# The down product of a feed-forward block as seven block products instead of eight

## The chip, the core and the metric

The kernel runs on one core of a Trainium2 chip. A core has a matrix engine (TensorE, PE in the profile), a vector engine (VectorE, DVE), an activation engine (ScalarE, ACT), a general engine (GpSimd, POOL) and a queue engine that issues transfers (SyncE, SP). Each runs its own instructions in order and waits on semaphores for the others. The metric is the time of one execution on the device in microseconds (us).

## The reference

One decoder layer on 1024 tokens of width 1024, in float32: an attention branch and a spatial-gating branch are merged by gates and projected, then comes the feed-forward block, of which the last two lines concern this change.

```python
merged = gate_a * (attn @ w_proj_attn[l]) + gate_b * (sgu @ w_proj_sgu[l])
x = x + merged @ w_out[l]
h2 = rmsnorm(x, norm2_g[l])
ff = jax.nn.silu(h2 @ w_ffn_gate[l]) * (h2 @ w_ffn_up[l])
x = x + ff @ w_ffn_down[l]          # 1024 x 2816 by 2816 x 1024
return rmsnorm(x, final_g)
```

## The kernel before

A float32 operand is held as a high part and a rest (`split`, L102 to L104: ACT copies the high part, DVE subtracts it). Every product of two tiles is three matmuls: high by high, rest by high, high by rest. H holds split activations; WH and WL are the two halves of a ring of eight slots of 512 columns for split weights.

The stages that matter follow each other on TensorE:

- **Gates** (L791 to L825): two phases of eight column tiles c. For each, `gate` (24 matmuls, sigmoid on ACT) and `proj` (12 matmuls, multiplied from PSUM by DVE, L811 or L813) run in turn for the two halves of the tokens. `proj` uses two PSUM banks in turn. The pool tag `att` (two buffers of 128 x 1024) belongs to the attention outputs, the last of which is stored before the gates.
- **Out-projection** (L968 to L980): two column halves; in the second, the eight token tiles T go in the order 0, 1, 4, 2, 5, 3, 6, 7. After each, `h2_do` adds, normalises (square on ACT, rstd on POOL, multiply on DVE), stores the sum x2 in DRAM and plans, six slots later, the tile's transposes: `first_H` for T below 4, `combine_H` for T of 4 and more. `combine_H` (L864) forms the sums of blocks that gate and up need, since those are already computed as 2x2 block products with seven products instead of eight, and splits them into H and HX. After the loop, the first five weights of gate/up are split and the transposes still planned are issued, tile 7's among them.
- **Gate/up** (L997): the list `order` gives 154 products (f, i) of 12 matmuls, f one of 22 column tiles of the hidden width and i one of 7 block products; splits of weights are issued five products ahead. A finished tile of activations ffo[f], 128 hidden columns by 1024 tokens, is stored to DRAM by POOL (L959).
- **Down** (L1017 to L1078): for each half ch of the output columns, for each f: load ffd[f] (512 KB) and 512 columns of the weight row block (256 KB), split them, and multiply for eight token tiles into eight PSUM banks, three matmuls each. `down_operands` is called three steps ahead. The last four f go tile by tile, so that a tile's addition, norm and output run beside the next tile. The eight x2 tiles are loaded at the start of the stage, in one block on SyncE.

Instructions are written in this order, but the framework's scheduler sets the final order on each engine.

Of the kernel before, what the change touches and what calls it, by code (L numbers as in the profile page):

```python
# [55 lines left out]
def hybrid_block(ctx: ExitStack, tc: tile.TileContext, x, positions, norm1_g, w_in, sgu_ln_g, sgu_ln_b,  # L56
# [12 lines left out]
    def close_pool(cm):  # L69
# [5 lines left out]
            "sm": 8, "cmb": 2, "x2": 8, "y": 2, "gr": 6, "sn": 5, "e": 4, "ffo": 2, "ffr": 3, "wdr": 4, "yo": 3, "c": 5}  # L75
    PBUFS = {"acc": 3, "tr": 2, "s": 2, "o": 1, "X": 3, "Y": 2, "V": 2, "Z": 1, "d": 8}
# [786 lines left out]

    def combine_H(y, T):  # L864

        a, b = tok_of(T - 4), tok_of(T)
        ps = [PS("tr"), PS("tr")]
        for kt in range(KT):
            nc.tensor.transpose(ps[kt // 4][:, kt % 4 * P:(kt % 4 + 1) * P], y[:, kt * P:(kt + 1) * P], ident)
        a21, a22 = k4(T_("c", [P, 512])), k4(ps[1])  # L870
        nc.scalar.copy(a21, k4(ps[0]))
        a11, a12 = (k4(x2[T - 4][:, half_of(h)]) for h in range(2))
        s1, s2, s3 = (k4(T_("c", [P, 512])) for _ in range(3))
# [11 lines left out]
    def h2_do(T):  # L885
# [3 lines left out]
        at(cur[0] + 6, lambda: (first_H if T < 4 else combine_H)(t, T))  # L889

    ring = [0]
    ffd = [dram.tile([P, S], F32, name=f"ffd{f}") for f in range(NF)]
# [31 lines left out]

    def product(f, i):
# [19 lines left out]
        if i == 7:  # L945
            ffo[f] = row_tile([P, S])
# [11 lines left out]
        if i == (4 if f == NF - 1 else 3):  # L958
            nc.gpsimd.dma_start(out=ffd[f], in_=ffo.pop(f))  # L959

    order = [(f, i) for f in range(3) for i in (1, 2)]
    order += [(0, 6), (0, 5), (0, 7), (1, 6), (0, 4), (0, 3), (1, 5), (1, 7), (2, 6), (1, 4), (1, 3), (2, 5), (2, 7),
              (3, 1), (2, 4), (3, 2), (2, 3)]
# [4 lines left out]
    for ch in range(2):  # L968
        for kp in range(4):
            need(("o", ch, kp))  # L970
        for T in (range(NT) if ch == 0 else (0, 1, 4, 2, 5, 3, 6, 7)):
# [5 lines left out]
            if ch == 1:  # L977
                h2_do(T)
            if ch == 1 and T in (2, 3, 7):
                load_gu((2, 3, 7).index(T))  # L980
    for n in range(5):
        weights(*order[n])
    for n in sorted(sched):
        for f in sched.pop(n):
            f()
    close_pool(out_pool)
    close_pool(first_psum)

# [7 lines left out]
    AHEAD_W = 5  # L996
    for n, (f, i) in enumerate(order):  # L997
        if n + AHEAD_W < len(order):
            weights(*order[n + AHEAD_W])
        product(f, i)  # L1000
        if i == 7:
            load_gu(f + 3)
    close_pool(gu_pool)
# [9 lines left out]
    outs = [T_("yo", [P, D]) for _ in range(3)]  # L1013
    ops = {}
    place = [0]

    def down_operands(ch, f):  # L1017
        r = T_("ffr", [P, 2, 512])
# [87 lines left out]
```

## Time and profile before

| what | value |
| --- | --- |
| median of 3 runs | 1755.47 us (1755.43 to 1755.71) |
| the profiled execution | 1754.95 us, of which the span from first to last instruction is 1753.2 us |
| TensorE clock granted, mean over the span | 0.990 |
| moved by DMA | 160.65 MB, mean 92 GB/s |
| 22 stores of ffd | 512 KB each, issued by POOL |
| 44 loads of ffr, 44 of wdr | 512 KB and 256 KB each, issued by SyncE |

The profile's page gives busy time by engine, the span in 40 slices, DMA queues, the chain of work that ended last, and groups of like instructions with their mean duration and what ended the idle time before them. Matmuls overlap: a matmul's own duration is longer than the distance from its start to the next one's start. The views by window, by order of time and by chain of waits come from the same execution.

### The profile page before, as it was taken

To read this page: it belongs to the slowest core of one execution; us is meant where nothing else is said; L and a number is where in the kernel's file an instruction comes from. 1 tells how busy PE (TensorE), PEld (TensorE's weight loads), DVE (VectorE), ACT (ScalarE), POOL (GpSimd) and SP (SyncE) were. 2 spreads that over 40 slices of the span, in tenths; PEclk is the share of its full clock that TensorE was granted. 3 is DMA by queue.
4 is the path that set the end of the run, shared out by engine and by line. 5 is a ranking of instruction groups with operands and counts; after the bars stand their busy time and mean duration, and the time that the engine had idled before them with its cause. 6 is when DMAs were issued, how large, how long until landed. Compare 5 with 4: busy or idle time off the path is not lost.

```text
span 1753.2 us, 21816 instructions
## 1 busy us (share of the span) xinstructions
PE 1713.5 (98%) x8338; PEld 1391.3 (79%) x8338; DVE 838.5 (48%) x1582; ACT 646.9 (37%) x1253; POOL 164.7 (9%) x287
## 2 busy tenths in 40 slices
PE   8999999999999999999999998999999999899997
PEld 7877877877877778888888876888888887688886
DVE  5365375366456664212324268545555553543432
ACT  5344445434435543212213055333333332432323
POOL 6200120030030141000000020000000000000003
PEclk9999999999999999999999998999999999999999
DMA  7312321342151232112312233222223211853522
GB/s 210 90 40 66 103 78 52 83 111 63 29 147 37 47 83 63 48 37 65 89 51 77 104 125 92 89 91 73 73 88 93 72 49 71 319 193 101 189 75 96
DMA packets 167256, 160.65 MB, mean 92 GB/s; under 512 B 10992, under 2 KB 138352, under 8 KB 167152
## 3 DMA queue, kind: packets, MB, share of 16 engines
q1 hardware_dynamic: 143152, 123.24, 22.6%
q0 software_dynamic: 8640, 26.58, 4.7%
q10 hardware_dynamic: 15360, 9.45, 2.3%
q8 instruction: 65, 1.06, 0.2%
q14 instruction: 39, 0.32, 0.1%
HBM read 127.54 MB, written 28.54 MB: 89 GB/s over the span
## 4 chain that ended last, share of the span: by engine, by line
PE 48%; issue 25%; DMA 2%; POOL 1%; DVE 1%; ACT 1%; ACTq 0%; POOLq 0%; DVEq 0%; SPq 0%
PE ps_acc L376 5%; PE ps_acc L377 5%; PE ps_acc L378 5%; PE ps_d L1034 4%; PE ps_d L1035 4%; PE ps_d L1036 4%; PE ps_acc L364 4%; PE ps_acc L363 4%; PE ps_acc L365 4%; PE ps_s L377 2%; PE ps_s L378 2%; PE ps_s L376 2%; PE ps_s L463 2%; PE ps_tr L490 1%; PE ps_o L512 1%
## 5 line engine op out<-in xcount | busy, mean ns | idle before, releaser
L376 PE MATMUL ps_acc<-H,WH 128*128 128x512 f32 x640 | 254.1, 397 | 0.0
L378 PE MATMUL ps_acc<-H,WL 128*128 128x512 f32 x640 | 253.6, 396 | 0.0
L377 PE MATMUL ps_acc<-H,WH 128*128 128x512 f32 x640 | 253.4, 396 | 0.0
L103 ACT CAST WH<-raw 128x512 fp32r<-128x512 f32 (+2 forms) x176 | 136.5, 778 | 289.6 <-PE ps_acc L377 91.9
L104 DVE TENSOR_TENSOR WL<-raw,WH 128x512 fp32r<-128x512 f32 (+2 forms) x176 | 155.0, 883 | 119.2 <-ACT WH L103 118.3
L363 PE MATMUL ps_acc<-WH,H 128*128 128x384 f32 (+1 forms) x512 | 190.7, 374 | 2.4 <-ACT H L103 2.4
L365 PE MATMUL ps_acc<-WH,H 128*128 128x384 f32 (+1 forms) x512 | 190.8, 373 | 0.5 <-DVE H L104 0.5
L364 PE MATMUL ps_acc<-WL,H 128*128 128x384 f32 (+1 forms) x512 | 189.0, 370 | 0.4 <-DVE WL L104 0.4
L1034 PE MATMUL ps_d<-WH,H 128*128 128x512 f32 x352 | 134.8, 395 | 7.7 <-ACT WH L103 7.7
L378 PEld LDWEIGHTS ps_acc<-H,WL 128*128 128x128 f32 x640 | 120.6, 188 | 27.0 <-issue 0.3
L376 PEld LDWEIGHTS ps_acc<-H,WH 128*128 128x128 f32 x640 | 120.5, 188 | 27.0 <-issue 1.2
L377 PEld LDWEIGHTS ps_acc<-H,WH 128*128 128x128 f32 x640 | 120.6, 188 | 25.9 <-issue 0.5
L1035 PE MATMUL ps_d<-WH,H 128*128 128x512 f32 x352 | 135.1, 391 | 0.0
L1036 PE MATMUL ps_d<-WL,H 128*128 128x512 f32 x352 | 134.5, 389 | 0.0
L481 ACT ACTIVATE S<-S,sm 128x128 f32<-128x128 f32 (+1 forms) x192 | 84.9, 445 | 80.6 <-DVE sm L479 75.3
L363 PEld LDWEIGHTS ps_acc<-WH,H 128*128 128x128 f32 x512 | 97.0, 190 | 14.9 <-ACT H L103 2.9
L365 PEld LDWEIGHTS ps_acc<-WH,H 128*128 128x128 f32 x512 | 97.1, 190 | 13.0 <-issue 1.0
L364 PEld LDWEIGHTS ps_acc<-WL,H 128*128 128x128 f32 x512 | 96.9, 189 | 11.9 <-DVE WL L104 1.0
L935 PE MATMUL ps_X<-H,WH 128*128 128x512 f32 x264 | 104.2, 395 | 0.7 <-ACT sn L940 0.7
L936 PE MATMUL ps_X<-H,WH 128*128 128x512 f32 x264 | 104.2, 395 | 0.0
L937 PE MATMUL ps_X<-H,WL 128*128 128x512 f32 x264 | 101.1, 393 | 0.0
L104 DVE TENSOR_TENSOR WL<-rows,WH 128x512 fp32r<-128x512 f32 x66 | 45.5, 692 | 110.4 <-ACT WH L103 110.4
(248 smaller groups left out, 2910.9 us busy)
## 6 DMA issues: line engine op xcount, KB each, us to landing
raw<-in_w_in_dram SPq DMA_DIRECT2D x48, 512.0 KB
ffr<-ffd SPq DMA_DIRECT2D x44, 512.0 KB
rows<-in_w_ffn_gate_dram SPq DMA_DIRECT2D x22, 512.0 KB
rows<-in_w_ffn_up_dram SPq DMA_DIRECT2D x22, 512.0 KB
ffd<-rows POOLq DMA_DIRECT2D x22, 512.0 KB, 2.9
wdr<-in_w_ffn_down_dram SPq DMA_DIRECT2D x44, 256.0 KB
raw<-in_w_in_dram SPq DMA_DIRECT2D x32, 192.0 KB
vd<-vst ACTq DMA_DIRECT2D x96, 64.0 KB
```

The costliest lines, as they stand in the source:

```text
L103: nc.scalar.copy(hi, src)
L104: return tt(out=lo, in0=src, in1=fb(hi), op=ALU.subtract)
L363: mm(o, H[:, 0, kt, tok], wh, start=(kt == 0), stop=False)
L364: mm(o, H[:, 0, kt, tok], wl, start=False, stop=False)
L365: mm(o, H[:, 1, kt, tok], wh, start=False, stop=(kt == KT - 1))
L376: mm(ps, WH[:, w], rh[:, half_of(half)], start=(kt == 0), stop=False)
L377: mm(ps, WH[:, w], rl[:, half_of(half)], start=False, stop=False)
L378: mm(ps, WL[:, w], rh[:, half_of(half)], start=False, stop=(kt == n - 1))
L935: mm(ps, WH[:, w], OPS[i](0, k), start=first and k == 0, stop=False, skip_group_check=True)
L1034: mm(ps, at_(0, T), wh, start=f == 0, stop=False)
L1035: mm(ps, at_(1, T), wh, start=False, stop=False)
L1036: mm(ps, at_(0, T), wl, start=False, stop=f == NF - 1)
```

## The change

**The algebra.** The hidden width is taken in eleven pairs p of tiles (2p even, 2p + 1 odd), the tokens and the output columns in halves. Of each pair the activations are A11, A21 (even tile, first and second half of the tokens) and A12, A22 (odd tile), the weights B11, B12 (even rows, column halves) and B21, B22 (odd rows). Seven products, each summed over the eleven pairs, replace eight: A11 B11; A12 B21; S2 T2; S1 T1; S3 T3; S4 B22; A22 T4, with S1 = A21 + A22, S2 = S1 - A11, S3 = A11 - A21, S4 = A12 - S2, and T1 to T4 alike from the weights (the code holds -T4's sign in the weight). The running sums stay in PSUM: products 1, 6, 7, 4 in the four banks X, products 2 and then 5, 3 in the four banks V, read by DVE after each product into the quarter of x2 that needs them.

**Where it is put.** The weight sums (`combine_wd`) are formed in the gates in the two `att` buffers: load on POOL, four subtractions on DVE, store on POOL into twd, one pair for each of eleven column tiles. The sums of activations (`ff_done`, `ff_s4`) are formed in gate/up and stored in five pieces per pair. Down has 77 steps of 12 matmuls with two loads of 256 KB and two splits of 512 columns each; an x2 tile is loaded in each of the first eight steps. Tiles 0 to 3 are normalised during the last product, tiles 4 to 7 at its end. The first three steps' operands are loaded and split while gate/up still runs.

**Also moved.** The out-projection takes T in the order 0, 4, 1, 5, 2, 6, 3, 7, plans transposes seven slots later, loads gate/up's weights after T = 1, 2, 3, and leaves tile 7's `combine_H` to gate/up, behind the second product, in PSUM banks V and tiles sn.

```diff
+    def load_wd(p):
+        if p < NP:
+            wd_raw[p] = [T_("att", [P, D]) for _ in range(2)]
+            for j, t in enumerate(wd_raw[p]):
+                nc.gpsimd.dma_start(out=t, in_=w_ffn_down[0, (2 * p + j) * P:(2 * p + j + 1) * P, :])
+    def combine_wd(p):
+        if p < NP:
+            a, b = wd_raw.pop(p)
+            b0, b1 = half_of(0), half_of(1)
+            tt(out=a[:, b0], in0=a[:, b1], in1=a[:, b0], op=ALU.subtract)
+            tt(out=a[:, b1], in0=b[:, b1], in1=a[:, b1], op=ALU.subtract)
+            tt(out=b[:, b1], in0=b[:, b1], in1=a[:, b0], op=ALU.subtract)
+            tt(out=b[:, b0], in0=b[:, b0], in1=b[:, b1], op=ALU.subtract)
+            for j, t in enumerate((a, b)):
+                nc.gpsimd.dma_start(out=twd[p][j], in_=t)
+            load_wd(p + 1)
...
                 proj(0)
+                combine_wd(8 * ph + c - ph)
                 gate(1)
...
+        if T == NT - 1:
+            return t
-        at(cur[0] + 6, lambda: (first_H if T < 4 else combine_H)(t, T))
+        at(cur[0] + 7, lambda: (first_H if T < 4 else combine_H)(t, T))
...
+    def ff_done(f):
+        d = pair_d[f // 2]
+        if f % 2 == 0:
+            return put(d["a11"], ffo[f][:, t0])
+        e, o = ffo[f - 1], ffo[f]
+        put(d["o"], o)
+        s1 = T_("sn", [P, 512])
+        tt(out=s1, in0=e[:, t1], in1=o[:, t1], op=ALU.add)
+        tt(out=e[:, t1], in0=e[:, t0], in1=e[:, t1], op=ALU.subtract)
+        tt(out=e[:, t0], in0=s1, in1=e[:, t0], op=ALU.subtract)
+        put(d["s1"], s1)
+        put(d["e"], e)
+    def ff_s4(f):
+        e, o = ffo.pop(f - 1), ffo.pop(f)
+        s4 = o[:, t0] if f < NF - 1 else T_("sn", [P, 512])
+        tt(out=s4, in0=o[:, t0], in1=e[:, t0], op=ALU.subtract)
+        put(pair_d[f // 2]["s4"], s4)
...
-        for T in (range(NT) if ch == 0 else (0, 1, 4, 2, 5, 3, 6, 7)):
+        for T in (range(NT) if ch == 0 else (0, 4, 1, 5, 2, 6, 3, 7)):
...
+    steps = [(i, p) for i in (1, 2, 6, 5, 7, 3, 4) for p in range(NP)]
+    SIDE = {1: ("a11", 0), 2: ("o", 0), 6: ("e", 0), 5: ("s1", 0), 7: ("e", 1), 3: ("s4", 0), 4: ("o", 1)}
...
+    def down_operands():
+        n = next_op[0]
+        next_op[0] += 1
+        i, p = steps[n]
+        side, c = SIDE[i]
+        r = T_("raw" if n < 3 else "ab", [P, 2, 512])
+        nc.sync.dma_start(out=r[:, 0], in_=pair_d[p][side][:, half_of(c)])
+        nc.sync.dma_start(out=r[:, 1], in_=down_weight(i, p))
+        hi, lo = (H[:, j, n % 8, t0] for j in range(2))
+        split(hi, lo, r[:, 0])
+        a = ring[0] % 8 * 512
+        ring[0] += 1
+        split(WH[:, a:a + 512], WL[:, a:a + 512], r[:, 1])
...
     for n, (f, i) in enumerate(order):
+        if n == 1:
+            product(f, i)
+            combine_H(last_y, NT - 1)
         if n + AHEAD_W < len(order):
             weights(*order[n + AHEAD_W])
+        elif n - len(order) in (-3, -2, -1):
+            down_operands()
...
+    adds = {1: [(0, 0)], 2: [(0, 0)], 6: [(0, 1)], 5: [(1, 1)], 7: [(1, 1)], 3: [(0, 1)], 4: [(1, 0)]}
+    for n, (i, p) in enumerate(steps):
+        bank = V if i in (2, 5, 3) else X
+        while next_op[0] < min(n + 4, len(steps)):
+            down_operands()
...
+                down(bank[t], n, t, first, last)
+        if i == 1 and p < NT:
+            nc.sync.dma_start(out=x2[p], in_=x2d[p])
...
+                for h, c in adds[i]:
+                    xs = x2[4 * h + t][:, half_of(c)]
+                    tt(out=xs, in0=xs, in1=bank[t], op=ALU.add)
+                if final:
+                    norm_out(4 + t)
+        if i == 4 and p in (1, 2, 3, 4):
+            norm_out(p - 1)
```

The order on TensorE at the end of the out-projection, before. ps_acc is its PSUM bank, ps_tr a bank of transposes (L214 `first_H`, L869 `combine_H`), and ps_X the first product of gate/up:

```order
L365 MATMUL ps_acc_8466<-WH_67,H_66 128x512
L869 MATMUL ps_tr_8371<-ident_69,raw_8341 128x128 x4
L869 MATMUL ps_tr_8372<-ident_69,raw_8341 128x128 x4
L214 MATMUL ps_tr_8438<-ident_69,raw_8404 128x128 x4
L214 MATMUL ps_tr_8446<-ident_69,raw_8404 128x128 x4
L869 MATMUL ps_tr_8488<-ident_69,raw_8458 128x128 x4
L869 MATMUL ps_tr_8489<-ident_69,raw_8458 128x128 x4
L869 MATMUL ps_tr_8543<-ident_69,raw_8521 128x128 x4
L869 MATMUL ps_tr_8544<-ident_69,raw_8521 128x128 x4
L935 MATMUL ps_X_8582<-H_66,WH_67 128x512
```

The same place in the change (L897 is `combine_H`, L990 the first matmul of a product):

```order
L365 MATMUL ps_acc_8648<-WH_67,H_66 128x512
L214 MATMUL ps_tr_8564<-ident_69,raw_8519 128x128 x4
L897 MATMUL ps_tr_8606<-ident_69,raw_8573 128x128 x4
L897 MATMUL ps_tr_8607<-ident_69,raw_8573 128x128 x4
L214 MATMUL ps_tr_8673<-ident_69,raw_8636 128x128 x4
L214 MATMUL ps_tr_8681<-ident_69,raw_8636 128x128 x4
L990 MATMUL ps_X_8718<-H_66,WH_67 128x512
```

Tile 7's transposes, the last two rows of L869 before, are gone from here; they stand 24 matmuls later, and tile 3's are now the last ahead of the first product.

The order on SyncE as down begins, in the change, with what each row waits for. ab is the buffer of a step's operands from step 3 on, ff_a block A11 of a pair, x a tile of x2. DMAHW and DMASW count finished transfers of SyncE and of POOL; DMASW6 is there the store of the last pair's combined tile e, DMASW7 that of its S4:

```order
L1065 DMA ab_11682<-ff_a_3_8005 128x512 [waits DMAHW2_49,DMAHW1_49,DVE_49]
L1066 DMA ab_11682<-in_w_ffn_down_dram 128x512
L1152 DMA x_1386_11661<-x2d_7982 128x1024 [waits DMAHW3_49,PE_49]
L1065 DMA ab_11702<-ff_a_4_8010 128x512 [waits DMAHW4_49,DMASW6_49,DVE_49]
L1066 DMA ab_11702<-in_w_ffn_down_dram 128x512 [waits DMAHW5_49]
L1152 DMA x_1387_11662<-x2d_7983 128x1024 [waits DMAHW6_49]
L1065 DMA ab_11722<-ff_a_5_8015 128x512 [waits DMASW7_49,DMASW5_49,DMAHW7_49,DMASW4_49,DMASW3_49]
L1066 DMA ab_11722<-in_w_ffn_down_dram 128x512 [waits DMAHW0_49]
L1152 DMA x_1388_11663<-x2d_7984 128x1024 [waits DMAHW1_49]
```

Before, the eight x loads stood in one block behind the third step's operands; now one stands behind each step's two loads, and the load of step 4 stands behind the store of e, whose old buffer its own overlays.

The order on DVE in the gates, before. L811 multiplies a bank of `proj`, and WL is the rest of a split weight:

```order
L811 TENSOR_TENSOR A_6490<-S_6516,ps_s_6518 128x512
L104 TENSOR_TENSOR WL_68<-raw_6397,WH_67 128x512
L811 TENSOR_TENSOR A_6490<-S_6561,ps_s_6563 128x512
L104 TENSOR_TENSOR WL_68<-raw_6468,WH_67 128x1024
L811 TENSOR_TENSOR A_6490<-S_6606,ps_s_6608 128x512
```

The same place in the change, where L836 is that multiply and L807 to L810 are the four subtractions on a pair's two att buffers:

```order
L807 TENSOR_TENSOR att_6881<-att_6881 128x512
L808 TENSOR_TENSOR att_6881<-att_6882,att_6881 128x512
L809 TENSOR_TENSOR att_6882<-att_6882,att_6881 128x512
L836 TENSOR_TENSOR A_6536<-S_6562,ps_s_6564 128x512
L810 TENSOR_TENSOR att_6882<-att_6882 128x512
L104 TENSOR_TENSOR WL_68<-raw_6433,WH_67 128x512
L807 TENSOR_TENSOR att_6982<-att_6982 128x512
L836 TENSOR_TENSOR A_6536<-S_6617,ps_s_6619 128x512
L104 TENSOR_TENSOR WL_68<-raw_6514,WH_67 128x1024
L808 TENSOR_TENSOR att_6982<-att_6983,att_6982 128x512
```

The subtractions now stand ahead of multiplies and weight splits, and each pair's first one waits for a load.

More of the change, by code (lines that the diff above doesn't have):

```diff
@@ L945, in product @@
         if i == 7:
+            if f % 2 == 0 and f:
+                ff_s4(f - 1)
             ffo[f] = row_tile([P, S])
@@ L977, in hybrid_block @@
             if ch == 1:
[L978 to L982, printed above, removed]
+                last_y = h2_do(T)
+                if T in (1, 2, 3):
+                    load_gu(T - 1)
     for n in sorted(sched):
@@ L996, in hybrid_block @@
     AHEAD_W = 5
+    done_at = {(f, max((3, 4), key=lambda i: order.index((f, i)))) for f in range(NF)}
+    late.update(bank="V", tile="sn")
     for n, (f, i) in enumerate(order):
+        if n == 1:
+            product(f, i)
+            combine_H(last_y, NT - 1)
         if n + AHEAD_W < len(order):
             weights(*order[n + AHEAD_W])
-        product(f, i)
+        elif n - len(order) in (-3, -2, -1):
+            down_operands()
+        if n != 1:
+            product(f, i)
         if i == 7:
             load_gu(f + 3)
+    ff_s4(NF - 1)
     close_pool(gu_pool)
@@ L1012, in hybrid_block @@
     fgb = T_("fgb", [P, D])
[L1013 to L1018, printed above, removed]
-        nc.sync.dma_start(out=r, in_=ffd[f].rearrange("p (h t) -> p h t", h=2))
-        w = T_("wdr", [P, 512])
-        nc.sync.dma_start(out=w, in_=w_ffn_down[0, f * P:(f + 1) * P, half_of(ch)])
-        j = place[0] % 8
-        place[0] += 1
-        rows, cols = slice(j % 4 * 2, j % 4 * 2 + 2), half_of(j // 4)
-        split(H[:, 0, rows, cols], H[:, 1, rows, cols], r)
-        a = ring[0] % 8 * 512
-        ring[0] += 1
-        split(WH[:, a:a + 512], WL[:, a:a + 512], w)
-        ops[ch, f] = (lambda i, T: H[:, i, j % 4 * 2 + T // 4, half_of(j // 4)][:, tok_of(T % 4)]), a
@@ new lines, in hybrid_block, with down @@
+    outs = [T_("yo", [P, D]) for _ in range(4)]
+    V = [PS("dv")]
+    X = [PS("dX") for _ in range(4)]
+    V += [PS("dV") for _ in range(3)]
+    def down(ps, n, t, first, last):
+        at_, a = ops[n]
+        tok = slice(t * P, (t + 1) * P)
+        wh, wl = WH[:, a:a + 512], WL[:, a:a + 512]
+        mm(ps, at_[0][:, tok], wh, start=first, stop=False, skip_group_check=True)
+        mm(ps, at_[1][:, tok], wh, start=False, stop=False, skip_group_check=True)
+        mm(ps, at_[0][:, tok], wl, start=False, stop=last, skip_group_check=True)
@@ new lines, in hybrid_block @@
+    TAIL = 4
+    for n, (i, p) in enumerate(steps):
+        bank = V if i in (2, 5, 3) else X
+        while next_op[0] < min(n + 4, len(steps)):
+            down_operands()
+        first, last = p == 0 and i in (1, 2, 5), p == NP - 1
+        final = i == steps[-1][0]
+        if not final or p < NP - TAIL:
+            for t in range(4):
+                down(bank[t], n, t, first, last)
+        if i == 1 and p < NT:
+            nc.sync.dma_start(out=x2[p], in_=x2d[p])
+        if (i, p) == (2, 0):
+            bcast(fgb, final_g)
+        if last:
+            for t in range(4):
+                if final:
+                    for m in range(n - TAIL + 1, n + 1):
+                        down(bank[t], m, t, False, m == n)
+                for h, c in adds[i]:
+                    xs = x2[4 * h + t][:, half_of(c)]
+                    tt(out=xs, in0=xs, in1=bank[t], op=ALU.add)
+                if final:
+                    norm_out(4 + t)
+        if i == 4 and p in (1, 2, 3, 4):
+            norm_out(p - 1)
```

101 lines of the change are left out of this document (45 added, 56 removed).

## The prediction

> **What bounds the kernel now.** I read the page's totals first, then a table by stage, then the order of time at the seams between stages.
>
> ```profile
> span 1753.2 us, 21816 instructions
> PE 1713.5 (98%) x8338; PEld 1391.3 (79%) x8338; DVE 838.5 (48%) x1582; ACT 646.9 (37%) x1253; POOL 164.7 (9%) x287
> ```
>
> TensorE (PE) is busy nearly throughout, and no other engine passes half. The table by stage gives the busy time of each engine and its instructions, then clock, DMA share and GB/s:
>
> ```profile
> core 0: us, PE busy (x) PEld busy (x) DVE busy (x) ACT busy (x) POOL busy (x), PEclk, DMA share, GB/s
> 700.00:880.00 180.00, 180.00 (x793) 148.01 (x792) 45.41 (x61) 35.28 (x54) 0.00 (x0) 1.00 0.20 60
> ...
> 1048.20:1063.70 15.50, 6.44 (x33) 4.51 (x32) 15.06 (x25) 11.36 (x22) 1.35 (x3) 0.69 0.45 137
> 1063.70:1082.10 18.40, 18.40 (x74) 15.06 (x73) 17.27 (x30) 9.75 (x16) 0.00 (x0) 0.89 0.20 57
> 1082.10:1488.00 405.90, 405.90 (x1761) 330.21 (x1760) 209.34 (x327) 140.35 (x247) 11.27 (x21) 1.00 0.24 76
> 1492.60:1525.00 32.40, 24.70 (x98) 19.77 (x98) 14.09 (x17) 12.84 (x18) 1.07 (x2) 0.89 0.90 330
> 1525.00:1700.00 175.00, 175.00 (x774) 144.91 (x773) 73.00 (x80) 56.12 (x72) 0.00 (x0) 1.00 0.48 158
> 1742.50:1753.20 10.70, 0.16 (x1) 0.00 (x0) 3.01 (x4) 2.48 (x4) 3.94 (x6) 0.72 0.46 172
> ```
>
> In gates (700), gate/up (1082) and down (1525) TensorE never pauses. What a matmul costs there is its pitch, not its 389 ns of busy time: 175.00 / 774 = 0.226 us. Time is lost at two seams only, out-projection to gate/up (1048) and gate/up to down (1492), and in the tail. So a matmul removed is worth 0.226 us if its operands still come in time, and a wait at a seam is worth its own length.
>
> ```profile
> 1047.99 0.39 PE L365 MATMUL ps_acc<-WH,H 128*128 128x512 f32 x1
> ...
> 1063.74 0.78 PE L935 MATMUL ps_X<-H,WH 128*128 128x512 f32 x1
> ...
> 1492.41 0.39 PE L937 MATMUL ps_X<-H,WL 128*128 128x512 f32 x1
> ...
> 1511.17 0.39 PE L1036 MATMUL ps_d<-WL,H 128*128 128x512 f32 x1
> 1517.13 0.79 PE L1034 MATMUL ps_d<-WH,H 128*128 128x512 f32 x1 [5.56 <-ACT WH L103]
> ...
> 1742.27 0.39 PE L1036 MATMUL ps_d<-WL,H 128*128 128x512 f32 x1
> ```
>
> **Part 1: the seven products.** Before, down issues 2 x 22 x 8 x 3 = 1056 matmuls, after, 7 x 11 x 4 x 3 = 924; the order lists 924. From the last gate/up matmul (1492.41) to the last down matmul (1742.27) are 249.9 us; 1056 x 0.226 = 238.8 are matmuls, 11.1 are lost at the seam. 924 x 0.226 = 208.9: **-29.9 us**. It needs operands every 12 matmuls, 2.71 us. The splits, down stage of before:
>
> ```profile
> L104 DVE TENSOR_TENSOR H<-ffr,H 128x1024 fp32r<-128x1024 f32 x36 | 43.9, 1225 | 9.8 <-ACT H L103 9.7
> L104 DVE TENSOR_TENSOR WL<-wdr,WH 128x512 fp32r<-128x512 f32 x36 | 24.8, 691 | 79.9 <-ACT WH L103 76.1 <-DMA ffr<-ffd 3.3 <-PE ps_d L1035 0.4
> ...
> L103 ACT CAST H<-ffr 128x1024 fp32r<-128x1024 f32 x37 | 38.7, 1048 | 5.1 <-DMA ffr<-ffd 5.1
> L103 ACT CAST WH<-wdr 128x512 fp32r<-128x512 f32 x35 | 21.7, 621 | 114.2 <-PE ps_d L1035 114.2
> ```
>
> A step now needs two 512-wide splits, 1.4 us on DVE and 1.2 on ACT, half of 2.71. ACT's 114.2 us of waiting for TensorE say that splits run ahead until the ring is full; the ring still holds eight steps. Hidden. The 28 additions from PSUM into x2 (16 before) fall between them, 0.69 us each, and each bank is next written a whole product (11 steps, 30 us) later. Loads: 512 KB per 2.71 us is 193 GB/s, against 158 in the row at 1525. What the queue can do shows in the stretches where it catches up, and in two loads of activations (SyncE issues):
>
> ```profile
> 1505.00:1515.00 10.00, 6.56 (x29) 5.08 (x28) 0.96 (x2) 0.00 (x0) 0.00 (x0) 1.00 1.03 411
> 1520.00:1524.00 4.00, 4.00 (x16) 3.20 (x15) 3.80 (x5) 3.58 (x5) 0.00 (x0) 0.77 1.02 383
> ```
> ```profile
> 1520.48 0.33 SPq L1019 DMA_DIRECT2D ffr<-ffd  x1
> ...
> 1522.39 0.33 SPq L1019 DMA_DIRECT2D ffr<-ffd  x1
> ```
>
> 383 to 411 GB/s, 768 KB every 1.9 us: 193 fits, hidden behind the matmuls in the steady part, and uncovered only while the x2 tiles load too (part 2). A rule speaks against this part: the Trainium skill, page "DMA: Bandwidth & Descriptors", section "Anatomy of one DMA", fits 2.0 us plus the bytes at 436 GB/s to a DMA, and "Bandwidth" asks for 1 MiB per DMA. By it a 256 KB load takes an estimated 2.6 us, a step of two 5.2, and down would be some 190 us longer if loads went singly. The trace disagrees with that reading: at 1520 three quarters of a MB go by every 1.9 us.
>
> **Part 2: the seam before down.** The chain of waits there, in order of time:
>
> ```profile
> 1494.46 2.95 DMA ffd<-rows
> 1497.46 5.57 DMA ffr<-ffd
> ...
> 1505.31 10.17 DMA ffr<-ffd
> ```
>
> The last activations are stored, read back, and then queue behind eight x2 loads (4 MB): 11.1 us, part of it a slow clock (0.89). After, product 1 reads only block a11 of the even tiles, stored long before; steps 0 to 3 are loaded before gate/up ends. Step 4's load waits for the store of the last combined tile, as the order's waits show, and every later load of SyncE stands behind it. From the end G of the last gate/up matmul: silu and the last product take 1.9 us (in before 1492.6 to the store at 1494.46), three DVE operations and the issue 1.9 more, and the store, with three others (1.5 MB at 411 GB/s, 3.7 us): landed near G+7.4; load 2.9, splits 1.4: G+11.7. Steps 0 to 3 last 10.9 us, so about 1 us is lost; step 5 stands behind an x2 tile, the norm weights and its own load (about 2 us more), and each of the next seven needs 1.05 MB, 2.9 us at 360 GB/s against 2.71: 1.4. Together 4.3 in place of 11.1: **-6.8**. Bounds: 0 lost (-11.1), and as much as before (0).
>
> **Part 3: the seam after the out-projection.** DVE sets it (15.06 of 15.50 us busy), one 512-wide operation every 0.60 us:
>
> ```profile
> 1063.20 0.68 DVE L876 TENSOR_TENSOR c<-c,rows 128x512 f32<-128x512 f32 x1
> 1063.80 0.69 DVE L878 TENSOR_TENSOR c<-rows,c 128x512 f32<-128x512 f32 x1
> ```
>
> Tile 7's eight transposes leave the path, but gate/up now starts behind tile 3's, whose splits stand in the same DVE queue; DVE's work is the same. Counting DVE's rows in the new order from tile 3's addition at 0.60 us (1.20 for the 1024-wide), tile 6's second bank comes free 12 us after the last out-projection matmul; tile 3's last transposes follow, then gate/up: 12.5 instead of 15.5. The second product waits for tile 3's split at about 17, then tile 7's transposes take 1.2. The six products that need no combination end about 32 us behind, before 33.9 (1048.2 to 1082.1): **-1**, allowing for a slip. Bounds: -9 (all of the gap's idle time, 15.5 less 6.44) and +3 (five more DVE operations ahead of the start). Tile 7's combination is needed only by product 7 of the order, and DVE reaches it 5 us earlier. Issues that move: the gate/up weight loads follow tiles 1, 2, 3 on SyncE with nothing else queued; the fourth waits for tile 3's row buffer, and has 14 products (38 us) to land.
>
> **Part 4: the weight combinations in the gates.** 44 DVE subtractions at 0.60 are 26 us in a stage where DVE has 135 of 180 idle. But the order puts them early, in front of the multiplies that empty TensorE's PSUM banks and of the splits (WL) that TensorE multiplies by; DVE takes its rows in order, so a late load blocks both.
>
> ```profile
> L811 DVE TENSOR_TENSOR A<-S,ps_s 128x512 f32<-128x512 f32 x16 | 11.0, 688 | 74.5 <-PE ps_s L378 74.4
> ```
> ```profile
> ffd<-rows POOLq DMA_DIRECT2D x22, 512.0 KB, 2.9
> ...
> n<-in_norm_g_dram POOLq DMA_DIRECT2D x1, 512.0 KB, 4.3
> attd<-att POOLq DMA_DIRECT2D x8, 256.0 KB, 2.3
> ```
>
> A cycle is four subtractions 2.4, store 2.9, load 2.9 (as a store) to 4.3 (as the norm weights): 8.2 to 9.6 us; the order gives six cycles seven multiplies, 36 matmuls apart: 57 us, 9.5 each. So loads land about when expected. A multiply late by up to about 10 us costs nothing, since two PSUM banks take turns; eleven cycles late by 1 us just fill that. I take **+1**; bounds 0 and +15 (2.3 us late per cycle, 25 less 10). POOL's 33 more issues before the out-projection stand in front of nothing but the norm weights.
>
> **Part 5: gate/up and the tail.** Four more DVE operations per pair,
>
> ```profile
> L922 DVE TENSOR_TENSOR raw<-rows,raw 128x512 f32<-128x512 f32 x40 | 27.4, 685 | 0.1
> ```
>
> 2.7 us in 37, beside TensorE with DVE 52% busy (209 of 406): 0; without that cover 30. Stores grow from 1 to 1.75 MB per pair, 76 to 96 GB/s: 0. The tail, in order of time:
>
> ```profile
> 1742.70 0.69 DVE L1060 TENSOR_TENSOR x<-x,ps_d 128x512 f32<-128x512 f32 x1 [0.48 <-PE ps_d L1036]
> ...
> 1744.30 0.72 ACT L1073 ACTIVATE yo<-x,sm 128x512 f32<-128x512 f32 x1 [2.09 <-POOL sm L199]
> 1744.93 1.04 ACT L1065 ACTIVATE yo<-x 128x1024 f32<-128x1024 f32 x1
> ```
>
> The last tile's square waits 1.5 us behind tile 6's scale, itself held by POOL's multiply of tile 5. After, POOL multiplies nothing there; the last tile then scales on ACT and multiplies on DVE in turn, +0.6. Net **-1**; bounds -2 and +1.
>
> **Sum**: -29.9 - 6.8 - 1 + 1 + 0 - 1 = -37.7. Against the profiled execution, 1754.95 us (span 1753.2, and 1.75 around it that stay): 1717.3. The median of the runs, 1755.47, is 0.5 higher: 1717.8; I say **1718**.
>
> **The rivals.**
> A. Down's start is bound by DMA, since all its operands now come in rows of 2 KB. Down moves 158 GB/s at a share of 0.48, so 329 at most; two thirds of these bytes come in 4 KB rows, which reach 411, so the 2 KB third may go at 235 only (1/329 = 0.667/411 + 0.333/235). Then a step's 512 KB take 2.2 us, which still fits, but the eight steps with an x2 tile take 3.5, 0.8 over, where I counted 0.2: +5, and up to 4 for TensorE's slow clock after a longer wait: 1723 to 1727. Against it: 383 GB/s at 1520, where a third is in 2 KB rows.
> B. **Slower.** Loads in down do not overlap: two of 256 KB at 2.3 us (the row of attd) are 4.6 us a step, 77 x (4.6 - 2.71) = +145: 1863. It decides from 3.20 us a step (37.7 / 77 over 2.71). Against: the two issues at 1520, 768 KB in 1.9.
> C. DVE blocks the gates: loads of 8 us in the cycle give 13.3 us against 9.5, eleven times, 42, less 10 of slack: +32, 1750. Against: 60 GB/s and a share of 0.20 there.
> D. The change does not do what it says, and the time stays at 1755: the order's 924 matmuls speak against it.
>
> **How the numbers follow.** Forecast 0.74 (its own range 1708 to 1727: half way to the lower bounds of parts 2 and 3, -4 to -6 together, and part 2 or part 4 up to 9 worse); A 0.14; C 0.08 (half of it under 1735); B 0.03, D 0.01. The range is 1708 to 1733. About 0.2% (3.5 us) is what a measurement of this kernel can tell from no change. Faster 0.96 (the forecast, A and C), same 0.01 (D), slower 0.03 (B).
>
> **What would show it.** Part 1: pitch 0.226 in down and no wait for a load after the x2 tiles. Part 2: TensorE idle under 5 us between the last gate/up matmul and step 13. Part 3: a first gate/up matmul some 12 us behind the last of the out-projection. Part 4: 793 matmuls in 180 us of the gates, DVE waits for att loads short. Wrong if TensorE pauses in the gates, or loads of down come one step late throughout.

## The result, and the profile after

The changed kernel takes 1716.03 us (median of four runs, 1713.07 to 1717.17) against 1755.45 for the kernel before on the same chip: ratio 0.9776, 95% interval 0.9759 to 0.9793. The forecast was 1718, in a range of 1708 to 1733. The profiled execution is the fastest of the four, 1713.07 us, with a span of 1711.4. The page's first lines:

```profile
span 1711.4 us, 22153 instructions
...
PE 1679.3 (98%) x8206; PEld 1363.4 (80%) x8206; DVE 918.3 (54%) x1751; ACT 667.7 (39%) x1319; POOL 203.9 (12%) x361
```

TensorE has 132 instructions fewer, as the change says, and is still what the kernel waits for. The table by stage (the same columns as before), then TensorE's rows at the ends of the stages, in order of time:

```profile
700.00:880.00 180.00, 180.00 (x794) 148.05 (x794) 65.33 (x95) 36.06 (x55) 16.10 (x30) 1.00 0.46 152
1046.80:1058.80 12.00, 4.25 (x22) 2.97 (x20) 12.00 (x20) 9.56 (x18) 2.38 (x3) 0.64 0.36 115
1078.50:1484.40 405.90, 405.90 (x1761) 330.26 (x1760) 235.25 (x370) 142.39 (x250) 27.75 (x51) 1.00 0.30 97
1489.00:1525.00 36.00, 32.35 (x141) 25.95 (x140) 17.11 (x26) 13.76 (x23) 2.70 (x5) 1.00 0.90 327
1525.00:1690.00 165.00, 164.32 (x725) 135.94 (x725) 102.67 (x156) 79.82 (x139) 10.28 (x12) 1.00 0.63 209
```
```profile
1046.54 0.39 PE L365 MATMUL ps_acc<-WH,H 128*128 128x512 f32 x1
...
1058.77 0.78 PE L990 MATMUL ps_X<-H,WH 128*128 128x512 f32 x1
...
1488.83 0.39 PE L992 MATMUL ps_X<-H,WL 128*128 128x512 f32 x1
1489.06 0.39 PE L1116 MATMUL ps_dX<-WH,H 128*128 128x512 f32 x1
...
1502.10 1.20 PE L1116 MATMUL ps_dX<-WH,H 128*128 128x512 f32 x4 [2.01 <-ACT WH L103]
1503.14 1.08 PE L1117 MATMUL ps_dX<-WH,H 128*128 128x512 f32 x4
...
1506.76 0.50 PE L1116 MATMUL ps_dX<-WH,H 128*128 128x512 f32 x1 [1.64 <-ACT WH L103]
...
1703.51 0.39 PE L1118 MATMUL ps_dX<-WL,H 128*128 128x512 f32 x1
```

The gates and gate/up have as many matmuls per microsecond as before, with DVE and POOL busier beside them. The first down matmul follows the last one of gate/up at once; the pauses come 13 us later, and are short. The difference of the spans, between the same matmuls of both traces:

| stretch | before | after | difference | forecast |
|---|---|---|---|---|
| start to last out-projection matmul | 1047.99 | 1046.54 | -1.5 | +1 |
| to the first HX product | 34.12 | 31.97 | -2.2 | -1 |
| to the last gate/up matmul | 410.30 | 410.32 | 0.0 | 0 |
| to the last down matmul | 249.86 | 214.68 | -35.2 | -36.7 |
| to the end of the span | 10.93 | 7.89 | -3.0 | -1 |
| span | 1753.2 | 1711.4 | -41.8 | -37.7 |

What ends the pause at 1502 stands in the table of SyncE's waits, and in the rows of POOL (the store of e), SyncE (step 4's load) and ScalarE (its first split) in order of time:

```profile
SPq L1065 <- DMA ff_e<-rows: 14.9, 1, 14.9
```
```profile
1493.05 0.54 POOL L926 DMA_DIRECT2D ff_e<-rows  x1 [0.91 <-DVE rows L969]
...
1498.07 0.33 SPq L1065 DMA_DIRECT2D ab<-ff_a  x1
...
1500.74 0.62 ACT L103 CAST H<-ab 128x512 fp32r<-128x512 f32 x1 [9.85 <-DMA ab<-ff_a]
```

SyncE stands for 14.9 us until the store of the last e has let go of the buffer that step 4's load overlays, and ScalarE stands for 9.85 us until that load has landed. That is the wait which the forecast named; how much it is worth, and why it is there at all, the experiments show.

### The profile page after: what moved, and what is told of

Same layout as the page of the kernel before. It is cut to its first block, busy times and chain, and to the rows that moved or that the text cites. A ratio compares the mean times of both kernels' runs of the same rounds, so it can differ in the third digit from the quotient of the medians.

```text
span 1711.4 us, 22153 instructions
## 1 busy us (share of the span) xinstructions
PE 1679.3 (98%) x8206; PEld 1363.4 (80%) x8206; DVE 918.3 (54%) x1751; ACT 667.7 (39%) x1319; POOL 203.9 (12%) x361
## 4 chain that ended last, share of the span: by engine, by line
PE 48%; issue 24%; POOL 2%; DVE 1%; DMA 1%; ACT 1%; SPq 0%; POOLq 0%; ACTq 0%; DVEq 0%
PE ps_acc L376 5%; PE ps_acc L377 5%; PE ps_acc L378 5%; PE ps_acc L364 4%; PE ps_acc L363 4%; PE ps_acc L365 4%; PE ps_dX L1116 2%; PE ps_dX L1117 2%; PE ps_dX L1118 2%; PE ps_s L377 2%; PE ps_s L378 2%; PE ps_s L376 2%; PE ps_s L463 2%; PE ps_dV L1118 1%; PE ps_dV L1116 1%
## 5 line engine op out<-in xcount | busy, mean ns | idle before, releaser
L365 PEld LDWEIGHTS ps_acc<-WH,H 128*128 128x128 f32 x512 | 97.3, 190 | 12.8 <-issue 1.0
L364 PEld LDWEIGHTS ps_acc<-WL,H 128*128 128x128 f32 x512 | 96.8, 189 | 11.5 <-DVE WL L104 0.4
L990 PE MATMUL ps_X<-H,WH 128*128 128x512 f32 x264 | 104.5, 396 | 0.7 <-ACT sn L995 0.7
L103 ACT CAST WH<-rows 128x512 fp32r<-128x512 f32 x66 | 40.7, 622 | 129.9 <-PE ps_X L991 92.0
L104 DVE TENSOR_TENSOR WL<-ab,WH 128x512 fp32r<-128x512 f32 x74 | 51.1, 691 | 59.1 <-ACT WH L103 59.1
L103 ACT CAST WH<-ab 128x512 fp32r<-128x512 f32 x74 | 46.0, 621 | 76.3 <-PE ps_dV L1117 40.7
```

Source lines behind the costliest of these rows:

```text
L103: nc.scalar.copy(hi, src)
L104: return tt(out=lo, in0=src, in1=fb(hi), op=ALU.subtract)
L364: mm(o, H[:, 0, kt, tok], wl, start=False, stop=False)
L365: mm(o, H[:, 1, kt, tok], wh, start=False, stop=(kt == KT - 1))
L990: mm(ps, WH[:, w], OPS[i](0, k), start=first and k == 0, stop=False, skip_group_check=True)
```

## The experiments

Twelve kernels ran, one of them the changed kernel again. All on one table first: the stretches as above, and the median and ratio of each, against the kernel before in the same runs. "Front" is the time of the last out-projection matmul, "down" runs from the last gate/up matmul to the last down matmul, and "tail" from there to the end of the span.

| kernel | front | to HX product | down | tail | span | median | ratio (95%) |
|---|---|---|---|---|---|---|---|
| again | 1047.4 | 31.91 | 214.93 | 7.9 | 1712.4 | 1715.26 | 0.9777 (0.9763 to 0.9790) |
| moved | 1049.7 | 31.88 | 241.79 | 10.9 | 1744.6 | 1744.62 | 0.9945 (0.9931 to 0.9958) |
| notmoved | 1051.2 | 33.18 | 210.43 | 7.8 | 1713.0 | 1712.71 | 0.9763 (0.9750 to 0.9777) |
| ffrmid | 1047.4 | 34.29 | 243.33 | 10.9 | 1746.2 | 1747.97 | 0.9963 (0.9949 to 0.9976) |
| abmid | 1052.1 | 31.86 | 210.42 | 7.8 | 1712.5 | 1712.55 | 0.9762 (0.9749 to 0.9775) |
| best | 1048.9 | 31.88 | 209.43 | 7.8 | 1708.3 | 1710.55 | 0.9752 (0.9738 to 0.9766) |
| bestback | 1047.5 | 32.91 | 209.44 | 7.9 | 1708.0 | 1712.38 | 0.9768 (0.9755 to 0.9782) |
| nocomb | 1047.1 | 31.93 | 215.30 | 11.5 | 1716.2 | 1718.26 | 0.9793 (0.9779 to 0.9807) |
| nosub | 1047.8 | 31.88 | 214.75 | 7.8 | 1712.5 | 1715.23 | 0.9770 (0.9756 to 0.9784) |
| cyc2 | 1058.3 | 32.10 | 214.47 | 9.7 | 1724.9 | 1725.46 | 0.9820 (0.9806 to 0.9834) |
| eighth | 1049.3 | 31.98 | 244.12 | 7.9 | 1743.6 | 1744.83 | 0.9948 (0.9935 to 0.9962) |
| abone | 1052.0 | 31.94 | 384.49 | 12.8 | 1891.5 | 1891.25 | 1.0782 (1.0767 to 1.0796) |

Gate/up took 410.30 to 410.32 in all of them. Read the column "front" first: after, again, abmid, best, eighth and abone have the same code up to that matmul, and differ there by up to 5.5 us (1046.5 to 1052.1). Some 3.5 us of that arise early: at TensorE's 2800th recorded matmul, ahead of the gates, all fourteen traces stand between 499.4 and 502.9 us. So effects of 1 to 4 us are read from the stretch in which they happen; there two profiles of the same code agree within 0.3 us (down of after and of again, 214.68 and 214.93).

**The changed kernel again.** No edit.

> The changed kernel once more, unaltered, as the mark for the runs beside it: 1713 to 1717 us. Its stages tell how far one profile differs from another: if the tail (last down matmul to the end of the span) is a saving of the code, it is again near 7.9 us (before 10.9); if it was luck of the last stores, it is anywhere from 7.9 to 11.

The tail is 7.9 us again: it was not the luck of one execution.

**Seven products against eight.** The second piece of the edit keeps the additions into x2 as many as in the changed kernel.

```diff
-    steps = [(i, p) for i in (1, 2, 6, 5, 7, 3, 4) for p in range(NP)]
+    steps = [(i, p) for i in (1, 2, 6, 5, 7, 3, 3, 4) for p in range(NP)]
...
-        if last:
+        if last and (final or steps[n + 1][0] != i):
```

> The changed kernel with an eighth product in down: the block product of S4 and b22 (i = 3) is issued twice, with its own loads and splits, so down has 88 steps and 1056 matmuls again, and one block of the output is off by that product. Theory: a step costs TensorE's pitch alone, 12 x 0.226 = 2.71 us, eleven steps 29.9: 1744 to 1747. Rival (steps bound by their loads or splits): more than 33. Rival (the seam gave most of the gain): under 25.

Down grows by 244.12 - 214.68 = 29.4 us, 2.68 a step. The removed product was worth its matmuls to within 0.5 us, and the loads and splits of a step stay hidden at 221 GB/s:

```profile
1525.00:1690.00 165.00, 164.31 (x725) 135.72 (x724) 97.25 (x153) 77.05 (x133) 0.00 (x0) 1.00 0.68 221
```

**One operand tile in down.**

```diff
-            "sm": 8, "cmb": 2, "x2": 8, "y": 2, "gr": 6, "sn": 6, "e": 3, "yo": 4, "ab": 6, "c": 5}
+            "sm": 8, "cmb": 2, "x2": 8, "y": 2, "gr": 6, "sn": 6, "e": 3, "yo": 4, "ab": 1, "c": 5}
```

> The changed kernel with one operand tile in down in place of six, so that a step's two loads start only when the splits of the step before have read theirs, and no two steps' loads overlap. Theory (loads are hidden because they run ahead, each takes 2.3 us or more to land): a cycle of issue, 256 KB twice and two splits is 4.5 to 5.0 us against 2.71, 74 steps: +130 to +170, 1845 to 1885. Rival (one load ahead is enough, the queue's rate of 383 GB/s sets it): under 20 us more.

Down takes 170 us more, 4.99 us a step (384.49 / 77), and the median is 6 us above the expected range. Its table by stage, and ScalarE's waits in the same 50 us:

```profile
1600.00:1650.00 50.00, 35.60 (x116) 25.29 (x115) 12.79 (x20) 12.29 (x20) 0.00 (x0) 0.84 0.32 105
```
```profile
ACT H L103 <- DMA ab<-ff_e: 39.3, 10, 5.6
```

Ten steps in 50 us, and ScalarE waits 3.9 us in each for the load. This is rival B of the forecast made real: a step whose loads run alone costs 5.0 us (the forecast had 4.6), and five more tiles hide all of it. One step's load, from its issue to the copy on ScalarE that reads it:

```profile
1621.07 0.32 SPq L1065 DMA_DIRECT2D ab<-ff_e  x1
...
1624.32 0.62 ACT L103 CAST H<-ab 128x512 fp32r<-128x512 f32 x1 [4.00 <-DMA ab<-ff_e]
```

That is 3.25 us, and 2.66 in the next step (1626.29 to 1628.95). The Trainium skill, page "DMA: Bandwidth & Descriptors", section "Anatomy of one DMA", gives an estimated 2.6 us for 256 KB, from a fit to transfers that GpSimd issues. These loads, which SyncE issues, come out near it when a step's loads run alone. With six tiles a step of two such loads stays hidden behind 2.71 us of matmuls, so the figure sets no limit once loads overlap.

**The moved transposes, alone and taken back.** The first kernel is the kernel before with this part of the change only, the second the changed kernel without it. The edit of the first, cut to its core (the order of the first gate/up products, the place of gate/up's first weight loads and the buffer counts of two tags change with it); the second undoes these lines:

```diff
-        at(cur[0] + 6, lambda: (first_H if T < 4 else combine_H)(t, T))
+        if T == NT - 1:
+            return t
+        at(cur[0] + 7, lambda: (first_H if T < 4 else combine_H)(t, T))
...
-        for T in (range(NT) if ch == 0 else (0, 1, 4, 2, 5, 3, 6, 7)):
+        for T in (range(NT) if ch == 0 else (0, 4, 1, 5, 2, 6, 3, 7)):
...
+        if n == 1:
+            product(f, i)
+            combine_H(last_y, NT - 1)
```

> The kernel before with the moved transposes alone (order of the out-projection tiles, the seventh slot, the last tile's combination behind the first gate/up product, order of the first gate/up products), with the eight block products of down and no combinations. Theory: the move is worth what the seam of the changed kernel shows by itself, 2.2 us from the last out-projection matmul to the first HX product: 1752 to 1754. Rival: the move is worth more than that, because the changed kernel pays for its combinations in the same stretch: 1749 or less. Rival: it is worth nothing alone: 1755.

> The changed kernel with the transposes put back (out-projection tiles in the order of before, sixth slot, the last tile's combination ahead of gate/up, first gate/up products in the order of before); the seven products stay. Theory: 2 to 3 us more than the changed kernel of the same call, all of it between the last out-projection matmul and the first HX product (34.1 in place of 32.0). Rival: it is the same, and the 2 us were found elsewhere.

Both theories missed. The time of moved lies under the 1749 of its first rival, but not for that rival's reason: the seam is as short in the changed kernel (31.97) as in moved (31.88). The move alone wins 9.6 us by the medians (1754.24 to 1744.62), not 2, and taking it out of the changed kernel wins 2.5 (1715.26 to 1712.71) where it should have cost as much. The seam behaves as expected in both (34.12 to 31.88, 31.97 to 33.18). The rest is in down, which the move does not touch: 249.86 to 241.79 in the one, 214.68 to 210.43 in the other. SyncE's waits at the start of down, from 1488 us on (1490 in notmoved), of before, of notmoved and of moved. In moved no wait for a store is left there; the one for the store of f = 20 ends at 1486.4, 5.5 us ahead of the last gate/up matmul:

```profile
SPq L1019 <- DMA ffd<-rows: 9.7, 1, 9.7
```
```profile
SPq L1063 <- DMA ff_e<-rows: 11.5, 1, 11.5
```
```profile
SPq L1029 <- DVE H L104: 11.4, 9, 2.3
SPq L1029 <- DMA x<-x2d: 5.7, 3, 3.6
```

The tiles of down lie where HX and the eight row buffers of gate/up lay. A load into such a tile waits until what was there has been stored. The addresses in the compiled programs, counted in row buffers from the first of them (HX lies at -12 to -1), show which tile of down meets the last activations, the rows of f = 20 and 21:

```
            row of f=20   row of f=21   tile of down that lies there
before      2             1             2: second ffr, 1: third ffr
moved       2             7             2: second ffr, 7: none
after       6             5             6: ab of step 4, 5: ab of step 5
notmoved    4             3             4: ab of step 6, 3: ab of step 8
```

The row buffers are not handed out in a fixed round. Up to row 11 all four programs use the same ones; the loads of the third gate and up blocks (rows 12 and 13) take buffers 1 and 7 without the move, 7 and 1 with it, and from there on the orders differ. So the move also changes which operand load stands behind the last store. In before it was the third, in moved none; in the changed kernel without the move it was step 6, with the move step 4, and steps 0 to 3 cover 10.9 us only. In notmoved step 6's load waits until 1503.49, 4.5 us after the store of e was issued, and TensorE has no pause there. In before the third load was issued at 1497.46, 3.0 us after the last store (1494.46).

**Operand tiles allocated first.** If that is the reason, another place for the tiles must bring the same without any transposes moved. In the changed kernel (abmid), and in the kernel before (ffrmid), where the calls go ahead of fgb and outs likewise. The last rows stay where they were; abmid's six operand tiles lie at -3, 2, 1, 0, -2 and -1, the three ffr tiles of ffrmid at -4, -2 and -3:

```diff
     fgb = T_("fgb", [P, D])
+    down_operands()
     outs = [T_("yo", [P, D]) for _ in range(4)]
```

> The changed kernel with one line moved: the down stage's operand tiles (ab) are allocated ahead of its output tiles, so they lie on HX and on row buffers that are stored long before; nothing else differs. Theory (step 4's tile lies on the row buffer of the second-last tile's activations, whose store of e goes out last, so its load waits for that store): the wait of SyncE for ff_e and the 2 us that TensorE waits for step 4 and step 5 go, down (last gate/up to last down matmul) falls from 214.8 to 210.5, and the time is 4 us under the changed kernel: 1709 to 1712. Rival (the x2 loads in front set it): down stays within 1 us of 214.8 and the wait for ff_e turns into one for x2d.

> The kernel before with the same line moved: its operand tiles (ffr, wdr) ahead of norm weights and output tiles, with the eight products and the transposes where they were. Theory (the third load of activations shared a row buffer with the last tile, and the moved transposes alone won their 8 us in down because they changed which row buffer that was): down falls from 249.9 to about 242, the time to 1745 to 1748, without any transposes moved and any product dropped. Rival (the moved transposes won it in another way): 1754.

Both came as expected, but for a median of abmid 0.6 us over its range. Down falls to 210.42 in the one and to 243.33 in the other, the medians by 2.7 and 5.9 us (against 1715.26, and against 1753.89 of the same runs; the first of these is hardly more than the front's spread, and rests on the stretch). In abmid TensorE goes through the place where after stood idle; its rows there, and SyncE's first waits:

```profile
1504.44 1.07 PE L1119 MATMUL ps_dX<-WL,H 128*128 128x512 f32 x4
1505.35 1.07 PE L1117 MATMUL ps_dX<-WH,H 128*128 128x512 f32 x4
1506.26 1.07 PE L1118 MATMUL ps_dX<-WH,H 128*128 128x512 f32 x4
```
```profile
SPq L1065 <- PE ps_Z L992: 16.9, 1, 16.9
SPq L1066 <- DMA x<-x2d: 9.3, 7, 2.5
```

The first load now waits for the last reader of HX, which is a product ahead of the end of gate/up and early enough, and no wait for ff_e is left.

**The x2 loads spread, and the transposes once more.** The first kernel adds this to abmid; the second is the first with the transposes put back.

```diff
-        if i == 1 and p < NT:
-            nc.sync.dma_start(out=x2[p], in_=x2d[p])
+        if i in (1, 2) and p % 2 == 1 and p < 8:
+            T = 4 * (i - 1) + p // 2
+            nc.sync.dma_start(out=x2[T], in_=x2d[T])
```

> The changed kernel with its operand tiles allocated ahead of the output tiles, as in the run before, and the eight x2 loads spread over every second step of the first two products in place of one in each of the first eight steps. Theory (once the wait for the store of e is gone, loads of x2 cost nothing more, and what is left is 0.7 us that a split stands behind four additions of DVE): down stays at 210.4 within 0.5, time 1710 to 1714. Rival (x2 loads still cost something): down near 209.5, a microsecond less.

> The kernel of the run before (operand tiles first, x2 loads spread) with the transposes put back as they were before the change. Now no operand tile of down lies on a row buffer that is stored late, whichever buffers the rows take, so the row buffers no longer blur what the transposes are worth. Theory (the move is worth what its own seam shows): HX seam 33.2 in place of 31.9, down 209.4 again, 1.3 us slower than the kernel of the run before: 1711 to 1714. Rival (the move is worth more or less than that elsewhere): down or gate/up differs by 1 us or more.

The number of the first expectation's rival came: with the x2 loads spread, down is 1.0 us shorter still (209.43), and a pause of 0.7 us that the changed kernel and abmid have is gone. But the x2 transfers did not cause that pause. In abmid it belongs to step 11's split:

```profile
1520.20 0.63 ACT L103 CAST WH<-ab 128x512 fp32r<-128x512 f32 x1
```
```profile
1523.91 2.48 DVE L1163 TENSOR_TENSOR x<-x,ps_dX 128x512 f32<-128x512 f32 x4 [3.02 <-PE ps_dX L1119]
1526.31 0.68 DVE L104 TENSOR_TENSOR WL<-ab,WH 128x512 fp32r<-128x512 f32 x1
```
```profile
1527.05 0.50 PE L1119 MATMUL ps_dv<-WL,H 128*128 128x512 f32 x1 [0.68 <-DVE WL L104]
```

Its load had landed when ScalarE copied it at 1520.20. DVE then stood 3.0 us for the end of the first product, because its order has the four additions ahead of this WL; TensorE waited for it. In the compiled program of the kernel with the loads spread, that WL stands ahead of the additions. So 0.7 of the 1.0 us came with another order on DVE; what the other 0.3 are stays open. That leaves 0.5 us over 924 x 0.226. At 1710.55 us this kernel has the lowest median of all, 5 us under the changed one, as is its stretch (214.68 to 209.43). The second kernel beside the first shows the transposes by themselves, as its theory had it: 1.0 us in their seam (32.91 to 31.88, for 1.3 expected), down the same; by the medians 1.8, with intervals that overlap.

**The combinations in the gates.** Three kernels: without any of it (nocomb), with loads and stores but no subtractions (nosub), and with a longer cycle (cyc2).

```diff
-    load_wd(0)
...
-                combine_wd(8 * ph + c - ph)
...
-        return twd[p][j][:, half_of(c)]
+        return w_ffn_down[0, (2 * p + j) * P:(2 * p + j + 1) * P, half_of(c)]
```
```diff
-            tt(out=a[:, b0], in0=a[:, b1], in1=a[:, b0], op=ALU.subtract)
...
-            tt(out=b[:, b0], in0=b[:, b0], in1=b[:, b1], op=ALU.subtract)
```
```diff
             for j, t in enumerate((a, b)):
                 nc.gpsimd.dma_start(out=twd[p][j], in_=t)
+                nc.gpsimd.dma_start(out=twd[p][j], in_=t)
```

> The changed kernel without the weight combinations in the gates: no loads, subtractions and stores of blocks of the down weights there; the down product reads plain blocks of the same size in their place (the combined weights are left out of the computation). Theory: DVE's 44 subtractions and its 50 us of waits for loads lie beside TensorE, so the time is that of the changed kernel within 1.5 us, and the gates show 793 to 794 matmuls in 180 us. Rival (DVE blocks the gates): 3 us or more faster, with more matmuls in the 180 us.

> The changed kernel with the loads and stores of the combinations kept and their 44 subtractions left out (so the stored blocks are plain blocks of the down weights, and the product of combined weights is left out of the computation). Theory (the combinations cost nothing in the gates, and the 3 us that the kernel without any combinations was slower by lay behind the last store, where SyncE waited for TensorE's sequencer): same time as the changed kernel within 1.5 us, 1713 to 1717, the same 791 to 794 matmuls in the 180 us of the gates, and a tail of 7.9 us again. Rival (plain weights make it slower): 3 us more, in the tail.

> The changed kernel with each combined weight block stored twice to the same place, one store behind the other, so that a cycle of the combinations in the gates (load, four subtractions, store) grows by one store of 512 KB, about 3.3 us, from the 11.0 us it has between 728 and 783 us of the changed kernel's profile to about 14.3. Theory (the 1 to 1.5 us by which each cycle is longer than the 9.5 us given is taken out of TensorE's slack of about 10 us, which six to eleven such cycles nearly use up): TensorE now pauses in the gates, fewer than 785 matmuls in the 180 us, and the time is 10 to 30 us over the changed kernel, 1725 to 1745. Rival (there is more slack than that): the same within 2 us.

Leaving the combinations out gains little: the front is 1047.1 and 1047.8 beside 1046.5 and 1047.4 in after and again, and TensorE is busy throughout the 180 us of the gates in both, with 791 matmuls each. But they are not free in every execution. From the 2800th matmul to the last out-projection matmul, the five kernels without subtractions (before, moved, ffrmid, nocomb, nosub) take 547.1 to 547.5 us; with them, after, again, best and bestback take 547.1 to 547.6, and notmoved, abmid, eighth and abone 548.6 to 549.4. Those four show a wait of TensorE that after does not have, here of abone between 600 and 1046 us:

```profile
PE ps_tr L753 <- DVE A L743: 1.1, 2, 0.7
```

L743 is an operation of the spatial gating, and it stands on DVE behind subtractions of the combinations (in abone the first of them, at 658.03 us, had waited 0.9 us for its load). So the combinations cost between nothing and 2 us.

That nocomb is 3 us slower than again had not been expected; nearly all of it is in the tail, 11.5 us. SyncE's waits in the last 9 us, of nocomb and of after (the line is the end of the program in both):

```profile
SPq L1188 <- PEq L1188: 4.3, 2, 3.8
SPq L1188 <- DMA out_dram<-yo: 1.4, 2, 0.8
```
```profile
SPq L1190 <- DMA out_dram<-yo: 1.4, 2, 0.8
SPq L1190 <- PEq L1190: 0.7, 2, 0.5
```

In nocomb SyncE stands at the end for TensorE's instruction queue, whose last matmul was done 11 us before; with nosub, which reads the same plain weights, the tail is 7.8 again, so the product is not the cause. Nor is it the missing combinations alone: cyc2, which has them all, waits 2.0 us there, and its tail is 9.7. What delays that queue stays open.

The cycle that the forecast had set at 8.2 to 9.6 us is longer on the chip: its load takes 4.7 us (median) for the 2.9 to 4.3 given, its store 3.3 for 2.9. DVE's first subtraction of the sixth-last and the last cycle of after, then of two cycles of cyc2 that are seven apart:

```profile
727.69 0.69 DVE L807 TENSOR_TENSOR att<-att 128x512 f32<-128x512 f32 x1 [6.30 <-DMA att<-in_w_ffn_down_dram]
...
782.61 0.69 DVE L807 TENSOR_TENSOR att<-att 128x512 f32<-128x512 f32 x1 [6.33 <-DMA att<-in_w_ffn_down_dram]
```
```profile
720.08 0.69 DVE L807 TENSOR_TENSOR att<-att 128x512 f32<-128x512 f32 x1 [5.97 <-DMA att<-in_w_ffn_down_dram]
...
833.09 0.69 DVE L807 TENSOR_TENSOR att<-att 128x512 f32<-128x512 f32 x1 [9.55 <-DMA att<-in_w_ffn_down_dram]
```

54.92 / 5 = 11.0 us, and DVE waits 6 us of it for its load, yet TensorE does not pause in that stretch. At 16.1 us (113.01 / 7; the expectation had 14.3) it does: 755 matmuls in the 180 us, 39 fewer than 794, and 10 us lost by the medians. The table by stage of cyc2, and TensorE's waits in the same stretch:

```profile
700.00:880.00 180.00, 175.01 (x755) 142.37 (x754) 64.21 (x94) 33.81 (x54) 28.27 (x53) 0.98 0.64 214
```
```profile
PE ps_s L376 <- DVE A L837: 4.2, 2, 2.6
```

It is the mechanism of rival C: TensorE waits for the PSUM bank that DVE's multiply has yet to empty, because that multiply stands behind a load. These waits are most of the 5.0 us that TensorE is idle there; the rest of what 39 matmuls are worth (8.8 us) is a longer pitch, 175.01 / 755 = 0.232 us at a granted clock of 0.98. It begins somewhere between a cycle of 11.0 and one of 16.1 us.

## Why the prediction was right, point by point

- **Part 1, seven products (-29.9): right.** Putting the product back costs 29.4. The pitch in down is still 0.226 and nothing waits for a load behind the x2 tiles. The one pause in the steady part, 0.7 us at step 11, comes from DVE's order. Rival B is what happens with one tile, at 5.0 us a step for the forecast's 4.6.
- **Part 2, the seam before down (-6.8): right mechanism, too small a loss.** Step 4's load waited for the store of e, as forecast. "Landed near G+7.4" was the step that failed: with G at 1489.06, SyncE could issue the load at 1498.07, G+9.0, so e's store held its row for 5.0 us from its issue at 1493.05, and not 3.7. Step 4 then started 13.0 us behind G, for the 11.7 forecast. The pauses are 2.0 us before step 4 and 1.6 before step 5 (about 1 and 2 forecast), and 0.7 at step 11, which the forecast did not have; the 1.4 us that it gave to the steps with x2 loads are not to be seen as pauses. The sign of under 5 us idle came (4.3). The wait for the store is worth 4.3 us by abmid (214.68 to 210.42) and the spread x2 loads 1.0 more, 5.3 in all against best, where 4.3 were forecast; measured as the forecast did, over 924 x 0.226, it is 5.8. The term becomes -5.3. One reading of before was wrong: the load at 1497.46 does not read the last activations back. It is the third step's, whose data had been stored long before, and it waited because its tile lies on the last row stored. So more than half of the 11.1 us lost before came from the same cause that the forecast named for after only: ffrmid wins 6.5 us of it back by moving the tiles (249.86 to 243.33).
- **Part 3, the seam after the out-projection (-1): right, a little small.** The first gate/up matmul came 12.2 us behind the last of the out-projection (12.5 forecast), the first HX product at 31.97 (about 32). Against the 34.1 of before that is 2.2. In the changed kernel the move is worth 1.0 to 1.2 of it (best against bestback, after against notmoved); the other 0.9 (34.12 to 33.18) come without the move, and where from stays open. The place that set the move's effect on the time was not in the sum at all: the row buffers, +4.3 in the changed kernel and -8.1 in the kernel before.
- **Part 4, the combinations (+1): right within what the front varies.** They cost 0 to 2 us, in part at a place that the forecast did not name, the additions of the spatial gating. The cycle was mis-sized (11.0 for 8.2 to 9.6), and the sign "DVE waits for att loads short" did not come: they are 6 us long. That TensorE does not pause all the same means more slack than the 10 us given; that the two errors cancel is luck. Rival C needs cycles longer than 11 us.
- **Part 5, gate/up (0) and the tail (-1).** Gate/up is the same to 0.02 us. The tail is 3.0 shorter. Up to the end of the last computation it is 4.7 us (1703.51 to 1708.20), where before took 6.1 (1742.27 to 1748.39): -1.4 for the -1 forecast: the last tile's square no longer waits, and its scale and multiply run in turn, as worked out. The other 1.6 lie behind it, where the last store and the end of the program took 3.2 in place of 4.8. That stretch took up to 6.9 us in nocomb, and no step of the forecast dealt with it.
- **Rival A** (down's start bound by its loads) is refuted: its price rests on rows of 2 KB that go at 235 GB/s only, and from 1525 to 1690 us, where all of down's loads and output stores have such rows, the kernel moved 209 GB/s at a share of 0.63, an estimated 332 at full share. Spreading the x2 loads wins 1.0 us, most of it by DVE's order.

The sum came within 2 us of the median. In the profiles it is 4 us off, of which 2.5 are the front, whose spread is larger than that. That the rest comes so near is in part luck: down won 1.5 us less than forecast, the seam after the out-projection and the tail 3.2 more.

## What to carry to other kernels

Where one stage's tiles lie on another's, ask of each early load whose old contents it waits for, and put the operands that are needed first on what is free first; a line that only moves an allocation was worth 4.3 and 6.5 us of the stage here, and an unrelated move of work swung the same wait by 4 us one way and 8 the other. When undoing a part of a change gives the opposite of what the part gave alone, look for something that both share, here the handing out of buffers, before believing either number. Removing matmuls paid their pitch here (29.4 us for 29.9), with six operand tiles that let the loads overlap; with one tile the loads set the time.

## What the runs showed that was not expected

- The last store of a combined tile (512 KB) held its buffer for 5.0 us, with three other stores issued within 3 us of it; 22 stores of that size landed in 2.9 us (median) in the kernel before.
- The same code reached its last out-projection matmul between 1046.5 and 1052.1 us in six profiles; up to 2 us of that lie where DVE does the combinations.
- The end of the program can cost 3 us more for a reason outside the work: SyncE waited up to 3.8 us at a time for TensorE's instruction queue in nocomb, 2.0 in cyc2, 0.5 in after.
